# An expert stage whose rows run in passes of 64 and 32: one pass of 32 for experts with few rows, bias rows loaded by another engine, and the work between the passes regrouped

## The chip, the cores and the metric

The kernel runs on one core of one Trainium2 chip. The metric is the device time of the core in microseconds (us). Three runs of the kernel before gave 1849.51 to 1851.67 us, median 1851.08.

Engines are named as in the profile: PE is the matmul engine (PEld its weight loads, PEq its sequencer, which also takes the branches and the waits), DVE the vector engine, ACT the scalar engine, POOL the general engine, SP the engine that issues most DMAs.

## What is computed

One decoder layer over 512 tokens of width 1024. A dense part comes first (a token mixer and a cross-attention, each with a LayerNorm) and does not change. Then a mixture of experts and a last LayerNorm:

```
logits = x @ w_router + b_router            # 512 x 32
top_val, top_idx = top_k(logits, 4)         # every token goes to 4 of 32 experts
gate = softmax(top_val)
for each expert e, over its own tokens xi:
    gu = xi @ w_gu[e] + b_gu[e]             # 1024 -> 2048, interleaved gate and linear part
    h  = min(g,7) * sigmoid(1.702*min(g,7)) * (clip(l,-7,7) + 1)
    y[token] += gate * (h @ w_dn[e] + b_dn[e])
out = layer_norm(alpha * x + y)
```

How many rows an expert has follows from the inputs. With the inputs of the reference, in the order of the experts: 49, 68, 94, 45, 50, 119, 41, 117, 131, 65, 9, 83, 52, 80, 73, 31, 73, 22, 27, 67, 85, 38, 45, 42, 144, 15, 147, 49, 58, 72, 21, 36. So 6 experts have up to 32 rows (10, 15, 17, 18, 25 and 30), 11 have 33 to 64, 12 have 65 to 128, 3 have 129 to 160, and none has more.

## The kernel before

The 512 KB slabs of the experts' weights (16 for the up projection and 8 for the down projection of each expert) stream through a ring of 36 buffers; SP issues them in the order in which they are used, each as soon as its buffer is free. The rows of an expert are the stationary side of the matmuls, in groups of 64 or 32 columns, and the slabs stream past them, 512 columns at a time. Groups of 64 run two at a time on the array, groups of 32 four at a time.

`up` goes through the eight slab pairs in four quarters (`q`). Each quarter is a chain of nested branches on a register that holds the expert's row count: a pass of 64 for rows 0 to 63 always, a pass of 32 for rows 64 to 95 if there are over 64, another for rows 96 to 127 if over 96, and a pass of 64 for rows 128 to 191 if over 128. `down` does the same in two halves. In this text a block is one such chain with its branches, so an expert has four blocks of `up`, two of `down`, and one in `hidden`, which transposes the activated units in the same nested way.

The program is one long list without a loop; the instructions of experts that are not needed are jumped over. Where a branch skips matmuls, the path that skips them goes by a wait of PE for its own semaphore ("waits PE_49" in the listings below, EVENT_SEMAPHORE in the trace), so that all paths leave the block with the same count.

The order around it, for each `e`: the four quarters of `up(e)`, with hooks between them (`turn_units`: the transposes of `hidden` for expert `e-1`; `next_slots`: the routing matmuls `sl` for expert `e+2`), then the first half of `down(e-1)`, then `units(e)` on DVE and ACT and on PE the transposes of the next expert's tokens (`tokens`, tile `xt`, copied by ACT to `xe`), the second half of `down(e-1)`, and at last `rows_out(e-1)` and an indirect DMA that adds the rows to `based`. This order is written out by hand.

The bias of `up` is a matmul at the end of the fourth quarter, with `bgu` as its moving side. `bias_rows` builds `bgu` once before the first expert: two halves of 128 x 1024 are loaded, and each is split on ACT and DVE in a chain of casts and subtractions (tiles `bguraw` and `bgu`).

Of the kernel before, what the change touches and what calls it, by code (L numbers as in the profile page):

```python
# [111 lines left out]
class Trunk:  # L112
# [541 lines left out]

    def layer_norm(self, z, out, gb, add=None, keep=False):
# [4 lines left out]
        for i in range(2):  # L660
            nc.vector.bn_stats(st[:, i, :], half(z, i))
        nc.vector.bn_aggr(mv[:, 0:2], st)
        self.rstd_col(mv[:, 2:3], mv[:, 1:2])
        nc.vector.scalar_tensor_tensor(mv[:, 3:4], mv[:, 0:1], -1.0, mv[:, 2:3], op0=OP.mult, op1=OP.mult)
        for i in range(2):
            v = half(z, i)
            nc.scalar.activation(v, v, AF.Identity, bias=mv[:, 3:4], scale=mv[:, 2:3])
            u = half(out, i) if keep else v
            nc.vector.tensor_mul(u, v, half(gb[0], i))  # L669
            (add or nc.vector).tensor_add(half(out, i), u, half(gb[1], i))  # L670

# [401 lines left out]
    def tokens(self, rv):  # L1073

        nc, tc = self.nc, self.tc
        x = self.mx.tile([128, 8, 192], F32, name="xe", tag="xe", bufs=1)

        def some(c, n, src, first=0):
            nc.scalar.copy(x[:, :, c:c + n], self.turned(src, 8, "xt", first).rearrange("p (k t) -> p k t", t=n))  # L1079

        some(0, 64, self.xg[0:64])
        with tc.If(rv > 64):  # L1082
            some(64, 64, self.xg[64:128], 64)
            with tc.If(rv > 128):
                some(128, 64, self.more_x)
        return x
# [50 lines left out]
    def units(self, rv, b, bm, twice, between):  # L1137

        tc = self.tc
        g = self.mx.tile([128, 512], F32, name="mg", tag="mg", bufs=1)  # L1140
        l, l2, lx = [self.mx.tile([128, 512], F32, name=n, tag=n, bufs=1) for n in ("ml", "ml2", "mlx")]
        with tc.If(rv > 128):
            self.some_units(g, lx, *bm)
        self.some_units(g, l, b[0], b[1], twice)
        between()
        with tc.If(rv > 64):
            self.some_units(g[0:64], l2[0:64], b[2][0:64], b[2][64:128])
            with tc.If(rv > 96):
                self.some_units(g[64:128], l2[64:128], b[3][0:64], b[3][64:128])
        return l, l2, lx  # L1150

    def hidden(self, rv, l, l2, lx):

        nc, tc = self.nc, self.tc
        hs = self.mx.tile([128, 8, 192], F32, name="hs", tag="hs", bufs=1)

# [4 lines left out]
        some(0, 64, l)  # L1161
        with tc.If(rv > 64):  # L1162
            some(64, 32, l2[0:64])
            with tc.If(rv > 96):  # L1164
                some(96, 32, l2[64:128], 64)
                with tc.If(rv > 128):
                    some(128, 64, lx)
        return hs
# [12 lines left out]

    def down(self, rv, h, w, middle):
        tc = self.tc
        y, y2 = [self.ps("y", "y") for _ in range(2)]
        y3, yx = [self.ps("yx", "gu") for _ in range(2)]
        for q in range(2):
            ks = range(4 * q, 4 * q + 4)
            self.down_64(ks, y, h[:, :, 0:64], w)
            with tc.If(rv > 64):
                self.down_32(ks, y2, h[:, :, 64:96], w)  # L1190
                with tc.If(rv > 96):  # L1191
                    self.down_32(ks, y3, h[:, :, 96:128], w)
                    with tc.If(rv > 128):
                        self.down_64(ks, yx, h[:, :, 128:192], w)
            if q == 0:
                middle()
        return y, y2, y3, yx

    def rows_out(self, rv, few, p, route):

        nc, tc = self.nc, self.tc
        self.ys.reverse()
        y = self.ys[0]
        yx = self.mx.tile([64, 1024], F32, name="ysx", tag="ysx", bufs=1)
        gate = route[0][1]
# [7 lines left out]

        with tc.If(rv > 64):
            with tc.If(rv > 96):
                with tc.If(rv > 128):
                    for n in range(2):
                        t = yx[:, ts(n, 512)]
                        nc.scalar.copy(t, p[3][64 * n:64 * n + 64])
                        nc.scalar.mul(t, t, route[1][1])  # L1220
                sums(slice(96, 128), p[2])
            sums(slice(64, 96), p[1])
        nc.vector.tensor_copy(y[0:64, 0:512], p[0][0:64])
        nc.scalar.copy(y[0:64, 512:1024], p[0][64:128])  # L1224
        self.scatter(y, route[0][0])
# [3 lines left out]
    def bias_rows(self):  # L1229
# [3 lines left out]
        for h in range(2):  # L1233
            raw = p.tile([128, 2, 512], F32, name="bguraw", tag=("ysx", "hs")[h], bufs=1)
            for i in range(4):
                nc.sync.dma_start(raw[32 * i:32 * i + 32], self.a["bgu"][:, ts(h, 1024)].rearrange("e (j c) -> e j c", j=2))
            nc.vector.tensor_scalar(raw[:, 1], raw[:, 1], 1.0, None, op0=OP.add)
            t = p.tile([128, 2, 512], BF, name="bgu", tag="bgu", bufs=2)
            nc.scalar.copy(t, raw)
            for first in (32, 64):  # L1240
                for r in (slice(a, a + 32) for a in range(first, 96, 32)):
                    nc.vector.tensor_sub(raw[r], raw[r], t[r])
                    nc.scalar.copy(t[r], raw[r])
            self.bgu.append(t)

    def cond(self, c, *engines):
# [3 lines left out]
    def experts(self):  # L1250
        nc, tc, a = self.nc, self.tc, self.a
        p, cond = self.mx, self.cond
        PE, DVE, ACT, POOL = (mybir.EngineType.PE, mybir.EngineType.DVE, mybir.EngineType.Activation, mybir.EngineType.Pool)
        self.more_x = p.tile([64, 1024], F32, name="mrxg", bufs=1)
        nc.vector.memset(self.more_x, 0.0)
        self.ys = [p.tile([128, 1024], F32, name=f"ysb{i}", bufs=1) for i in range(2)]
        for y in self.ys:
            nc.vector.memset(y, 0.0)

# [21 lines left out]
        def more_gather(e):  # L1281
            with tc.If(rv[e][2] > 128):
                self.gather(self.more_x, route[e][1][0])

# [8 lines left out]
        n = len(self.ring["s"][0])  # L1293
        fetch(24)
        self.bias_rows()
        fetch(n - 24)
        more_gather(0)
        xs, ls = {0: self.tokens(rv[0][0])}, {}
        with tc.manual_schedule(engines={PE, DVE, ACT, POOL}):
            for e in range(33):  # L1300
# [29 lines left out]
                def own_units(between):  # L1330
                    if e < 32:
                        ls[e] = self.units(rv[e][1], *own, route[e][2], between)
                    else:
                        between()

                if e < 32:
                    own = self.up(rv[e][3], e, xs.pop(e), lambda h, k: slabs[e, h, k], {0: [turn_units], 1: [first_slots], 2: [next_slots]})
# [11 lines left out]
    def overflow(self):  # L1349
# [4 lines left out]
        with tc.If(rv > CAP):  # L1354
# [52 lines left out]
            with tc.For_i(0, total, 1):  # L1407
# [52 lines left out]
                y = p.tile([128, 1024], F32, name="oy", tag="ysx", bufs=1)  # L1460
                for n in range(2):
# [15 lines left out]
    FP = 0, 2  # L1477

    NRAW = 8, 14, 5
    W0, KF, MID = 2, 0, 6  # L1480
# [43 lines left out]
```

## Time and profile before

| what | value |
| --- | --- |
| median of three runs | 1851.08 us (1849.51 to 1851.67) |
| profiled execution, its own time | 1848.75 us |
| its span, from the first to the last instruction | 1847.0 us |
| dense part, up to the first matmul of `up(0)` | 615.4 us |
| `up(0)` to the first matmul of `up(1)` | 35.0 us |
| from there to the end of the last `down` | 1160.1 us |
| the rest: last rows, last LayerNorm, output | 36.5 us |
| PE busy over the span | 1673.8 us (91%) |
| mean DMA rate over the span | 273 GB/s |

The profiled execution took 1.75 us more than its span (what lies before the first and after the last instruction), and it lies 2.3 us under the median of the three runs.

### The profile page before, as it was taken

How to read it: one execution, taken by the hardware profiler on the slowest of the kernel's cores; microseconds unless marked ns; L12 is line 12 of the kernel's file. 1: busy time of each engine (PE TensorE's matmuls, PEld its weight loads, DVE VectorE, ACT ScalarE, POOL GpSimd, SP SyncE). 2: the span in 40 equal slices, each digit the busy share in tenths (PEclk: the TensorE clock that was granted, in tenths of full speed). 3: DMA queues.
4: the chain of work that ended last, by engine and by line, in shares of the span. 5: the costliest groups of instructions: out<-in, count | busy, mean ns of one | idle time of the engine just before them, and what ended most of it. 6: DMA issues, size and time to landing. Idle time of an engine off the chain costs nothing. (4 is left out here: it accounts for less than half of the span.)

```text
span 1847.0 us, 26521 instructions
## 1 busy us (share of the span) xinstructions
PE 1673.8 (91%) x9564; PEld 853.2 (46%) x9564; DVE 625.5 (34%) x1322; ACT 469.8 (25%) x906; POOL 293.9 (16%) x402
## 2 busy tenths in 40 slices
PE   8999999999999688999999989899999999999991
PEld 7766877868987333333333333333333333333330
DVE  7855777567565411111111211111112102121114
ACT  5577655335443211101101201110101101111001
POOL 1010002421002211211101121111111211011102
PEclk9999999999999799999999999999999999999996
DMA  5223323675236999999858899999999999678973
GB/s 171 91 69 109 105 81 123 221 225 173 83 123 219 351 391 346 396 374 383 305 186 267 325 375 395 364 372 382 392 401 382 376 392 354 229 284 328 399 270 120
DMA packets 149256, 504.87 MB, mean 273 GB/s; under 512 B 21648, under 2 KB 24240, under 8 KB 149040
## 3 DMA queue, kind: packets, MB, share of 16 engines
q1 hardware_dynamic: 131152, 459.33, 66.2%
q0 software_dynamic: 17024, 40.97, 7.6%
q8 instruction: 149, 2.44, 0.5%
q10 hardware_dynamic: 864, 1.57, 0.2%
q14 instruction: 67, 0.55, 0.1%
HBM read 486.84 MB, written 33.29 MB: 282 GB/s over the span
## 5 line engine op out<-in xcount | busy, mean ns | idle before, releaser
L1098 PE MATMUL gu<-raw,xe 128*64 128x512 f32 (+1 forms) x2624 | 518.0, 601 | 27.8 <-PEq L1191 5.1
L1098 PEld LDWEIGHTS gu<-raw,xe 128*64 128x64 f32 (+1 forms) x2624 | 158.2, 127 | 319.8 <-issue 292.9
L1173 PE MATMUL y<-raw,hs 128*64 128x512 f32 x920 | 211.1, 597 | 17.1 <-PEq L1121 4.3
L1133 ACT ACTIVATE mg<-mg 128x512 f32<-128x512 f32 (+1 forms) x55 | 34.7, 630 | 528.8 <-DVE mg L1132 524.4
L1012 DVE TENSOR_REDUCE gs<-sl 128x1 f32<-128x3 f32 x32 | 5.1, 161 | 478.3 <-PE sl L1010 478.3
L998 POOL TENSOR_SCALAR oh<-places,pm 128x192 bf16<-128x192 bf16 x128 | 98.7, 800 | 387.9 <-PE sl L1010 375.8
L1173 PEld LDWEIGHTS y<-raw,hs 128*64 128x64 f32 x920 | 71.1, 136 | 126.5 <-issue 91.1
L130 DVE TENSOR_TENSOR wlo<-raw,whi 128x1024 fp32r<-128x1024 f32 (+2 forms) x81 | 86.9, 1075 | 45.8 <-ACT whi L130 45.3
L1031 POOL DMA_INDIRECT based<-ysb,ixm x32 | 51.5, 1611 | 292.5 <-ACT ysb L1224 280.2
L130 ACT CAST whi<-raw 128x1024 fp32r<-128x1024 f32 (+2 forms) x81 | 75.3, 932 | 81.9 <-issue 17.3
L1098 PE MATMUL gu<-wlo,xe 128*64 128x512 f32 (+1 forms) x368 | 87.5, 594 | 3.1 <-PEq L1164 1.7
L1098 PE MATMUL gu<-whi,xe 128*64 128x512 f32 (+1 forms) x336 | 79.3, 599 | 7.5 <-DVE ysb L1211 2.1
L1025 POOL DMA_INDIRECT xg<-x2d,ixm x32 | 35.9, 1121 | 313.3 <-PEq L1082 179.3
L1132 DVE TENSOR_SCALAR mg<-gu 128x512 f32<-128x512 f32 (+1 forms) x52 | 35.8, 688 | 126.9 <-PE gu L1090 122.8
L1079 ACT COPY xe<-xt 128x512 f32<-128x512 f32 x50 | 27.8, 588 | 190.5 <-PE xt L1070 190.5
L1180 PE MATMUL y<-raw,hs 128*32 128x512 f32 x440 | 57.6, 598 | 0.0
L1211 DVE TENSOR_TENSOR ysb<-ysb,y 32x512 f32<-32x512 f32 x30 | 20.4, 680 | 103.1 <-ACT ysb L1210 103.0
L162 PE MATMUL g<-xTh,wlo 128*128 128x512 f32 x128 | 52.1, 407 | 2.8 <-DVE wlo L130 2.8
L1158 ACT COPY hs<-ht 128x512 f32<-128x512 f32 (+1 forms) x55 | 26.5, 510 | 106.8 <-PEq L1162 56.2
L160 PE MATMUL g<-xTh,whi 128*128 128x512 f32 x128 | 52.2, 408 | 0.0
L161 PE MATMUL g<-xTl,whi 128*128 128x512 f32 x128 | 51.8, 405 | 0.0
L1098 PEld LDWEIGHTS gu<-wlo,xe 128*64 128x64 f32 (+1 forms) x368 | 25.2, 125 | 49.0 <-issue 47.1
(495 smaller groups left out, 2776.9 us busy)
## 6 DMA issues: line engine op xcount, KB each, us to landing
raw<-in_wgu SPq DMA_DIRECT2D x406, 512.0 KB
raw<-in_wdn SPq DMA_DIRECT2D x230, 512.0 KB
wlo<-in_wgu SPq DMA_DIRECT2D x53, 512.0 KB
whi<-in_wgu SPq DMA_DIRECT2D x53, 512.0 KB
raw<-in_wt SPq DMA_DIRECT2D x27, 512.0 KB
whi<-in_wdn SPq DMA_DIRECT2D x13, 512.0 KB
wlo<-in_wdn SPq DMA_DIRECT2D x13, 512.0 KB
tgd<-tg POOLq DMA_DIRECT2D x16, 256.0 KB, 3.5
```

Source lines behind the costliest of these rows:

```text
L130: return nc.scalar.copy(hi, src).ins, (lo_eng or nc.vector).tensor_sub(lo, src, hi.bitcast(F32)).ins
L160: mm(out, w[0], x[0], start=start, stop=False)
L161: mm(out, w[0], x[1], start=False, stop=False)
L162: mm(out, w[1], x[0], start=False, stop=stop)
L998: self.nc.gpsimd.tensor_scalar(oh[:, b], self.places, self.pm[:, b, e:e + 1], None, op0=OP.is_equal)
L1025: return self.nc.gpsimd.indirect_dma_start(out=xg, out_offset=None, in_=self.x2d, in_offset=bass.IndirectOffsetOnAxis(ap=ix[:, 0:1], axis= ...
L1031: self.nc.gpsimd.indirect_dma_start(out=self.based, out_offset=bass.IndirectOffsetOnAxis(ap=ix[:, 0:1], axis=0), in_=y, in_offset=None, bo ...
L1098: mm(out(h, j), x[:, k], w(h, k)[:, ts(j, 512)], start=k == 0, stop=False)
L1132: nc.vector.tensor_scalar(g, pg, 7.0, None, op0=OP.min)
L1133: nc.scalar.activation(g, g, AF.Gelu_apprx_sigmoid)
L1173: self.nc.tensor.matmul(o[64 * n:64 * n + 64], h[:, k], w(k)[:, ts(n, 512)], start=k == 0, stop=k == 7)
L1180: self.nc.tensor.matmul(o[r:r + 32], h[:, k], w(k)[:, ts(n, 512)], start=k < 2, stop=k > 5)
```

## The change

It has six parts.

1. `up`, `units`, `hidden`, `down` and `rows_out` get an outer branch on 32 rows. Above 32 the nested passes run as before; up to 32 a single pass of 32 runs in the `Else`.
2. Rows 128 to 159 run in a pass of 32 (a further one up to 191) in place of one pass of 64.
3. From `e = 1` on, `turn_units` and `next_slots` both run after the second quarter of `up`; they ran after the first and the third.
4. `units` and the next expert's token transposes run ahead of `down`; they ran between its halves.
5. `bias_rows` loads its rows from ACT's queue and not from SP's, comes ahead of all 36 slabs and not behind the first 24, and its first half uses the tile `ysb`. Tiles `ysb`, `more_x` and `ysx` are merged, and the ring grows by two slabs (`NRAW`).
6. The last LayerNorm takes the sums of blocks 1 and 3 on ACT (`sums`), and all its last additions run on DVE; those of blocks 0 and 2 ran on POOL.

```diff
 def up(...):
     for q in range(4):
         ks = (2 * q, 2 * q + 1)
-            self.up_part(e, ks, 64, x[:, :, 0:64], w, two(b))
-            with tc.If(rv > 64):
-                self.up_part(e, ks, 32, x[:, :, 64:96], w, four(b[2]))
-                with tc.If(rv > 96):
-                    self.up_part(e, ks, 32, x[:, :, 96:128], w, four(b[3]))
-                    with tc.If(rv > 128):
-                        self.up_part(e, ks, 64, x[:, :, 128:192], w, two(bm))
+            with tc.If(rv > 32) as some:
+                self.up_part(e, ks, 64, x[:, :, 0:64], w, two(b))
+                with tc.If(rv > 64):
+                    self.up_part(e, ks, 32, x[:, :, 64:96], w, four(b[2]))
+                    with tc.If(rv > 96):
+                        self.up_part(e, ks, 32, x[:, :, 96:128], w, four(b[3]))
+                        with tc.If(rv > 128):
+                            self.up_part(e, ks, 32, x[:, :, 128:160], w, four(bm[0]))
+                            with tc.If(rv > 160):
+                                self.up_part(e, ks, 32, x[:, :, 160:192], w, four(bm[1]))
+            with some.Else():
+                self.up_part(e, ks, 32, x[:, :, 0:32], w, four(b[0]))
...
 def down(...):
-            self.down_64(ks, y, h[:, :, 0:64], w)
-            with tc.If(rv > 64):
+            with tc.If(rv > 32) as some:
+                self.down_64(ks, y, h[:, :, 0:64], w)
+                with tc.If(rv > 64):
...
-            if q == 0:
-                middle()
+            with some.Else():
+                self.down_32(ks, y, h[:, :, 0:32], w)
...
 def bias_rows(self):
-            raw = p.tile([128, 2, 512], F32, name="bguraw", tag=("ysx", "hs")[h], bufs=1)
+            raw = p.tile([128, 2, 512], F32, name="bguraw", tag="hs", bufs=1) if h else self.ys.rearrange("p (j c) -> p j c", j=2)
             for i in range(4):
-                nc.sync.dma_start(raw[32 * i:32 * i + 32], self.a["bgu"][:, ts(h, 1024)].rearrange("e (j c) -> e j c", j=2))
+                nc.scalar.dma_start(raw[32 * i:32 * i + 32], self.a["bgu"][:, ts(h, 1024)].rearrange("e (j c) -> e j c", j=2))
...
 def experts(self):
-        fetch(24)
         self.bias_rows()
-        fetch(n - 24)
+        fetch(n)
...
+                hooks = {1: [turn_units, next_slots]} if e else {0: [turn_units], 1: [first_slots], 2: [next_slots]}
...
-                    out = self.down(rv[f][3], h[f], lambda k: slabs[f, 2, k], lambda: own_units(next_tokens))
+                    own_units(next_tokens)
+                    out = self.down(rv[f][3], h[f], lambda k: slabs[f, 2, k])
...
 def finish(self):
-                self.layer_norm(z, out[b], gb, nc.gpsimd if b in self.FP else None)
+                self.layer_norm(z, out[b], gb, stats=self.sums if b % 2 else None)
...
+    def sums(self, mv, z, scratch):
+        nc = self.nc
+        nc.scalar.activation(scratch, z, AF.Identity, accum_out=mv[:, 0:1])
+        nc.vector.tensor_scalar(mv[:, 3:4], mv[:, 0:1], -1.0 / 1024, None, op0=OP.mult)
+        nc.scalar.activation(scratch, z, AF.Square, bias=mv[:, 3:4], accum_out=mv[:, 1:2])
+        nc.vector.tensor_scalar(mv[:, 0:1], mv[:, 3:4], -1.0, None, op0=OP.mult)
+        nc.vector.tensor_scalar(mv[:, 1:2], mv[:, 1:2], 1.0 / 1024, None, op0=OP.mult)
```

What the change makes of the program is seen at two places. The first is one block of `up` on PE. Before, it is this (64x512 is the pass of 64, 32x512 one of 32, `gux` the rows from 128 on; L1119, L1121 and L1123 are the branches on 64, 96 and 128 rows, and a row with "waits PE_49" is the skipping path of that branch):

```order
L1119 COMPARE_AND_BRANCH
L1098 MATMUL gu<-raw,xe 32x512 [waits DVE_49]
L1098 MATMUL gu<-raw,xe 32x512 x7
L1121 COMPARE_AND_BRANCH
L1098 MATMUL gu<-raw,xe 32x512 x8
L1123 COMPARE_AND_BRANCH
L1098 MATMUL gux<-raw,xe 64x512 x8
L1123 UNCONDITIONAL_BRANCH
L1123 UNCONDITIONAL_BRANCH [waits PE_49]
L1121 UNCONDITIONAL_BRANCH [waits PE_49]
L1119 UNCONDITIONAL_BRANCH [waits PE_49]
```

The eight matmuls of rows 0 to 63 stand ahead of these rows without a branch, and the last row is also the end of the block. After the change, the same block of PE ends like this (L1131 is the new branch on 32 rows, L1139 the one on 160, `gux` now in 32x512):

```order
L1139 COMPARE_AND_BRANCH
L1110 MATMUL gux<-raw,xe 32x512 x8
L1139 UNCONDITIONAL_BRANCH
L1139 UNCONDITIONAL_BRANCH [waits PE_49]
L1137 UNCONDITIONAL_BRANCH [waits PE_49]
L1135 UNCONDITIONAL_BRANCH [waits PE_49]
L1133 UNCONDITIONAL_BRANCH [waits PE_49]
L1110 MATMUL gu<-raw,xe 32x512 [waits DMAHW0_49]
L1110 MATMUL gu<-raw,xe 32x512 [waits DMAHW2_49]
L1110 MATMUL gu<-raw,xe 32x512 x2
L1131 UNCONDITIONAL_BRANCH
```

A branch on 32 rows (L1131) now stands at the head of the block, and behind the paths for more rows lie eight matmuls for up to 32 rows, which those paths must jump over; the path of the eight matmuls itself has no wait of PE for its own semaphore.

The second place is ACT's program just ahead of `up(0)`. Before, behind the four DMAs that write `based` comes the copy of the first expert's tokens (`xe<-xt`, on which the first matmul of `up(0)` waits), and the bias rows' casts come later:

```order
L1048 DMA based<-x2g 128x512 [waits DMAHW1_49,DVE_49]
L1079 COPY xe<-xt 128x8x64 [waits PE_49]
L1282 UNCONDITIONAL_BRANCH
L1247 TENSOR_LOAD number [waits Pool_49]
L1082 COMPARE_AND_BRANCH
L1084 COMPARE_AND_BRANCH
```

After the change, ACT has these rows in that place (DMAHW0 to DMAHW7 are semaphores of DMAs, shared by turns; the four `based` DMAs use DMAHW6, 7, 0 and 1):

```order
L1060 DMA based<-x2g 128x512 [waits DMAHW1_49,DVE_49]
L1266 DMA ysb<-in_bgu 32x1024 [waits DMAHW2_49,DMAHW6_49,DMAHW1_49,DMAHW0_49]
...
L1266 DMA ysb<-in_bgu 32x1024 [waits DMAHW7_49]
L1266 DMA ysb<-in_bgu 32x1024
L1266 DMA bguraw<-in_bgu 32x1024 [waits DMAHW3_49,Activation_49]
L1266 DMA bguraw<-in_bgu 32x1024 [waits DMAHW5_49]
L1269 CAST bgu<-ysb 128x1024 [waits DMAHW2_49,DMAHW7_49,DMAHW1_49,DVE_49]
L1266 DMA bguraw<-in_bgu 32x1024 [waits DMAHW0_49]
L1273 CAST bgu<-ysb 32x1024 [waits DVE_49] x2
L1266 DMA bguraw<-in_bgu 32x1024 [waits DMAHW3_49]
L1273 CAST bgu<-ysb 32x1024 [waits DVE_49]
L1091 COPY xe<-xt 128x8x64 [waits PE_49]
```

The loads of both halves and the whole chain of casts of the first half now stand ahead of the copy of the first expert's tokens, and the first load waits for the `based` DMAs.

## Rows read from the trace of the kernel before

**Rows 1.** Windows of core 0: busy time (instructions) by engine, PE clock, DMA share, GB/s.

```profile
615.40:650.40 35.00, 21.93 (x116) 8.37 (x117) 13.50 (x24) 10.86 (x12) 8.30 (x11) 0.79 1.01 374
650.40:1810.50 1160.10, 1066.11 (x6492) 374.55 (x6492) 190.46 (x401) 135.93 (x240) 177.51 (x207) 1.00 0.91 344
1810.50:1847.00 36.50, 0.00 (x0) 0.00 (x0) 18.32 (x29) 6.55 (x9) 11.35 (x13) 0.56 0.35 127
```

**Rows 2.** PE's waits from 650.4 to 1810.5: total us, times, longest us.

```profile
PE sl L1007 <- PEq L1121: 6.2, 10, 0.8
PE gu L1098 <- PEq L1121: 4.1, 9, 0.5
...
PE gu L1098 <- DMA raw<-in_wgu: 1.5, 4, 0.5
```

**Rows 3.** PE's timeline in experts 9 and 10: start, us, what, [idle before <-releaser].

```profile
1034.71 3.65 PE L1098 MATMUL gu<-raw,xe 128*64 128x512 f32 x16 [0.16 <-PEq L1119]
...
1047.60 1.92 PE L1180 MATMUL y<-raw,hs 128*32 128x512 f32 x16
```

**Rows 4.** Branch and semaphore instructions of the branch on 64 rows: count, ns min/median/max, first and last start.

```profile
L1119 PEldq COMPARE_BRANCH  x128: 65/208/3248, 618.0 to 1789.2; - x128
L1119 PEldq EVENT_SEMAPHORE  x68: 51/51/51, 622.4 to 1793.2; - x68
```

**Rows 5.** The page's DMA queue of instruction fetches: packets, MB, share of 16 engines.

```profile
q8 instruction: 149, 2.44, 0.5%
```

**Rows 6.** PE's timeline in `up(2)` (94 rows), one quarter.

```profile
701.48 5.51 PE L1098 MATMUL gu<-raw,xe 128*64 128x512 f32 x32 [0.46 <-PEq L1121]
```

**Rows 7.** PE's timeline in `up(8)` (131 rows), where a quarter ends.

```profile
939.06 3.65 PE L1098 MATMUL gux<-raw,xe 128*64 128x512 f32 x16
942.65 0.47 PE L1007 MATMUL sl<-VT,oh 128*128 128x8 bf16 x8
...
```

**Rows 8.** PE's timeline in `up(8)`, its transposes.

```profile
920.43 0.46 PE L1070 MATMUL ht<-ident,ml 64*128 64x64 f32 x4 [0.35 <-ACT hs L1158]
```

**Rows 9.** ACT's timeline around the start of `up(0)`.

```profile
610.13 4.43 ACTq L1048 DMA_DIRECT2D based<-x2g  x4
614.81 0.59 ACT L1079 COPY xe<-xt 128x512 f32<-128x512 f32 x1 [4.48 <-PE xt L1070]
632.89 1.04 ACT L1239 CAST bgu<-bguraw 128x1024 bf16<-128x1024 f32 x1 [17.50 <-DVE bguraw L1237]
...
638.95 1.04 ACT L1243 CAST bgu<-bguraw 32x1024 bf16<-32x1024 f32 x1 [1.28 <-DVE bguraw L1242]
```

**Rows 10.** DVE's timeline there.

```profile
619.03 0.91 DVE L1258 MEMSET ysb<- 128x1024 f32 x1 [3.14 <-DMA based<-x2g]
...
632.41 0.41 DVE L1237 TENSOR_SCALAR bguraw<-bguraw 128x512 f32<-128x512 f32 x1
```

**Rows 11.** PE's timeline there.

```profile
615.45 5.24 PE L1098 MATMUL gu<-raw,xe 128*64 128x512 f32 x10 [0.68 <-ACT xe L1079]
...
632.10 3.65 PE L1098 MATMUL gu<-raw,xe 128*64 128x512 f32 x16 [0.21 <-issue]
640.04 0.38 PE L1090 MATMUL gu<-bgu,esel 128*64 128x512 bf16 x1 [4.29 <-ACT bgu L1243]
647.00 1.01 PE L1090 MATMUL gu<-bgu,esel 128*64 128x512 bf16 x3 [6.58 <-ACT bgu L1243]
...
650.42 7.33 PE L1098 MATMUL gu<-raw,xe 128*64 128x512 f32 x32 [0.54 <-ACT xe L1079]
```

**Rows 12.** Windows as in rows 1: experts 10 to 23, and `up(18)` with `down(17)`.

```profile
1025.60:1487.10 461.50, 417.52 (x2518) 149.69 (x2514) 77.59 (x172) 56.12 (x99) 83.45 (x100) 1.00 1.00 382
...
1299.00:1325.90 26.90, 24.58 (x136) 9.52 (x137) 5.64 (x13) 3.55 (x7) 5.77 (x7) 1.00 1.02 395
```

**Rows 13.** The timeline of the last LayerNorm.

```profile
1826.33 1.25 POOL L670 TENSOR_TENSOR fo<-fz,gain 128x512 f32<-128x512 f32 x1
...
1841.17 0.69 DVE L670 TENSOR_TENSOR fo<-fz,gain 128x512 f32<-128x512 f32 x1
```

More of the change, by code (lines that the diff above doesn't have):

```diff
@@ L653, in gains, with layer_norm @@
         return t
-    def layer_norm(self, z, out, gb, add=None, keep=False):
+    def layer_norm(self, z, out, gb, keep=False, stats=None):
         nc = self.nc
@@ L659, in layer_norm @@
         mv = self.pst.tile([128, 4], F32, name="mv", tag="mv")
-        for i in range(2):
-            nc.vector.bn_stats(st[:, i, :], half(z, i))
-        nc.vector.bn_aggr(mv[:, 0:2], st)
+        if stats:
+            stats(mv, z, out)
+        else:
+            for i in range(2):
+                nc.vector.bn_stats(st[:, i, :], half(z, i))
+            nc.vector.bn_aggr(mv[:, 0:2], st)
         self.rstd_col(mv[:, 2:3], mv[:, 1:2])
@@ L669, in layer_norm @@
             nc.vector.tensor_mul(u, v, half(gb[0], i))
-            (add or nc.vector).tensor_add(half(out, i), u, half(gb[1], i))
+            nc.vector.tensor_add(half(out, i), u, half(gb[1], i))
+    def sums(self, mv, z, scratch):
[5 more added lines that the diff above has]
+        nc.vector.tensor_scalar(mv[:, 1:2], mv[:, 1:2], 1.0 / 1024, None, op0=OP.mult)
     def transpose_tok(self, x, b, xT):
@@ L1084, in tokens @@
             with tc.If(rv > 128):
-                some(128, 64, self.more_x)
+                some(128, 64, self.more[64:128], 64)
         return x
@@ L1142, in units @@
         with tc.If(rv > 128):
-            self.some_units(g, lx, *bm)
-        self.some_units(g, l, b[0], b[1], twice)
+            nc.vector.memset(lx[64:128], 0.0)
+            self.some_units(g[0:64], lx[0:64], bm[0][0:64], bm[0][64:128])
+            with tc.If(rv > 160):
+                self.some_units(g[64:128], lx[64:128], bm[1][0:64], bm[1][64:128])
+        with tc.If(rv > 32) as some:
+            self.some_units(g, l, b[0], b[1], twice)
+        with some.Else():
+            self.some_units(g[0:64], l[0:64], b[0][0:64], b[0][64:128])
         between()
@@ L1159, in some @@
                            self.turned(src, 4, "ht", first).rearrange("p (j h t) -> p j h t", j=4, h=2))
-        some(0, 64, l)
-        with tc.If(rv > 64):
[L1163 to L1167, printed above, removed]
+        with tc.If(rv > 32) as more:
+            some(0, 64, l)
+            with tc.If(rv > 64):
+                some(64, 32, l2[0:64])
+                with tc.If(rv > 96):
+                    some(96, 32, l2[64:128], 64)
+                    with tc.If(rv > 128):
+                        some(128, 32, lx[0:64])
+                        some(160, 32, lx[64:128], 64)
+        with more.Else():
+            some(0, 32, l[0:64])
         return hs
@@ L1180, in down_32, with down @@
                 self.nc.tensor.matmul(o[r:r + 32], h[:, k], w(k)[:, ts(n, 512)], start=k < 2, stop=k > 5)
-    def down(self, rv, h, w, middle):
+    def down(self, rv, h, w):
         tc = self.tc
@@ L1187, in down @@
             ks = range(4 * q, 4 * q + 4)
-            self.down_64(ks, y, h[:, :, 0:64], w)
[L1189 to L1194, printed above, removed]
-            if q == 0:
-                middle()
+            with tc.If(rv > 32) as some:
+                self.down_64(ks, y, h[:, :, 0:64], w)
+                with tc.If(rv > 64):
+                    self.down_32(ks, y2, h[:, :, 64:96], w)
+                    with tc.If(rv > 96):
+                        self.down_32(ks, y3, h[:, :, 96:128], w)
+                        with tc.If(rv > 128):
+                            self.down_64(ks, yx, h[:, :, 128:192], w)
+            with some.Else():
+                self.down_32(ks, y, h[:, :, 0:32], w)
         return y, y2, y3, yx
@@ L1201, in rows_out @@
         nc, tc = self.nc, self.tc
-        self.ys.reverse()
-        y = self.ys[0]
-        yx = self.mx.tile([64, 1024], F32, name="ysx", tag="ysx", bufs=1)
+        y, yx = self.ys, self.more[0:64]
         gate = route[0][1]
@@ L1212, in sums @@
             nc.vector.tensor_scalar(y[r], y[r], gate[r], None, op0=OP.mult)
[L1214 to L1224, printed above, removed]
+        with tc.If(rv > 32) as some:
+            with tc.If(rv > 64):
+                with tc.If(rv > 96):
+                    with tc.If(rv > 128):
+                        for n in range(2):
+                            t = yx[:, ts(n, 512)]
+                            nc.scalar.copy(t, p[3][64 * n:64 * n + 64])
+                            nc.scalar.mul(t, t, route[1][1])
+                    sums(slice(96, 128), p[2])
+                sums(slice(64, 96), p[1])
+            nc.vector.tensor_copy(y[0:64, 0:512], p[0][0:64])
+            nc.scalar.copy(y[0:64, 512:1024], p[0][64:128])
+        with some.Else():
+            sums(slice(0, 32), p[0])
         self.scatter(y, route[0][0])
@@ L1244, in bias_rows @@
             self.bgu.append(t)
+        nc.vector.memset(self.ys, 0.0)
     def cond(self, c, *engines):
@@ L1253, in experts @@
         PE, DVE, ACT, POOL = (mybir.EngineType.PE, mybir.EngineType.DVE, mybir.EngineType.Activation, mybir.EngineType.Pool)
[L1254 to L1258, printed above, removed]
+        self.more = p.tile([128, 1024], F32, name="more", bufs=1)
+        self.ys = p.tile([128, 1024], F32, name="ysb", bufs=1)
+        nc.vector.memset(self.more, 0.0)
         order = []
@@ L1282, in more_gather @@
             with tc.If(rv[e][2] > 128):
-                self.gather(self.more_x, route[e][1][0])
+                self.gather(self.more[64:128], route[e][1][0])
         def routing(e):
```

9 lines of the change are left out of this document (4 added, 5 removed).

## The prediction

> **What bounds the kernel now.** I read the windows by stage first. The dense part is the same in both kernels. In the expert stage PE is busy 1066 of 1160 us at a clock of 1.00, while DVE and ACT are busy a sixth and an eighth [rows 1]. Then PE's waits in that stage: behind data they are tiny (1.5 us in all for a matmul of `up` behind a slab), and the longer ones name PE's own sequencer, PEq, that is branches and semaphores [rows 2]. So the stage lasts as long as PE's passes plus the gaps between blocks, and I cost the change by these two. A third place is the start: around `up(0)` the window's clock is 0.79 and PE waits for the bias rows [rows 1, 11]. The windows also show a DMA share of 1.00 over experts 10 to 23 [rows 12]: the slabs come just in time there, which makes a rival below.
>
> **Prices.** A pass of 64 over a quarter of `up`, or a half of `down`, takes 3.65 us, a pass of 32 takes 1.92 [rows 3]: 1.73 apart. The pass of 64 is eight pairs that follow each other by about 0.44 us (3.65 less the 0.59 of the last, over seven). Where a block of up to 64 rows ends, PE idles 0.16 us behind the last matmul's end [rows 3], so start follows start by 0.75 us instead of 0.44: the drain costs 0.31. That path passes the semaphore wait on the branch on 64 rows, 68 times, four for each of 17 experts [rows 4]. Where a block of 65 to 96 rows ends, PE idles 0.46 us [rows 6], since that path must also jump over the next path's rows. Where all passes run (over 128) there is no idle time at all: 942.65 follows a pass that ends at 942.71 [rows 7]. A branch takes between 65 and 3248 ns, median 208 [rows 4].
>
> **The change part by part**, in us against the profiled execution:
>
> *Up to 32 rows, 6 experts: -55.* Six blocks, each 1.73 shorter, are 10.4. Their path has no wait of PE for itself, so six times 0.31 of drain goes too: 12.3 for an expert, 74 for six. Against that, each block now begins with a jump over all the larger passes, seven per expert with the transposes, 42 in all. A jump is hidden as long as matmuls are queued, here 1.92 us of them where before there were 3.65; the longest branch took 3.25, so a stall is between 0 and 1.33 us, 0 to 56 in all. I take 0.45 per jump, nearer to the median (208 ns, covered) than to the longest: 19. The term lies between -74 and -18.
>
> *33 to 64 rows, 11 experts: +33.* The same passes, but this path now ends like that of 65 to 96 rows, with a drain and a jump over the `Else`: 0.46 in place of 0.16. And every block begins with a branch not taken that comes right behind a drain, with nothing queued to hide it: at least 0.065, at most the median 0.208, I take 0.13. That is 0.43 for each of seven blocks (four, two, and `hidden`), 3.0 for an expert. Bounds +23 (the jump alone) to +39. A gain is excluded, for no matmul is removed.
>
> *65 to 128 rows, 12 experts: +8.* They only get that branch at the head of seven blocks: 84 times 0.065 to 0.208, +5.5 to +17; I take 0.1, since part of them follow blocks whose drain is longer.
>
> *Over 128 rows, 3 experts: -8.* Four passes of 64 become passes of 32: -6.9. But these blocks had no drain and no jump [rows 7], and now have both, about 0.6 in each of seven: +4.2. Net -2.7 each; between -21 (if blocks stay without gaps) and -8.
>
> *Transposes and slots in one place: +4.5.* The number of borders between kinds of work stays the same. But the slots now follow the transposes at once, and both use the same PSUM tiles, whose release is ACT's copy `hs`; such a wait took 0.35 [rows 8]. For 15 experts with over 64 rows 0.3 each; 0 to +9.
>
> *Tokens ahead of `down`: +2.* PE's own work is the same. The copies `xe` now have all of `down` as cover (at least 3.5 us) instead of half. A third transpose (three experts) waits for a copy that stands behind ACT's activation: 0.6 each; 0 to +4. If the cover were gone, a copy of 0.59 [rows 9] would show in front of `up`.
>
> *Bias rows: +4.5.* Now PE waits for them at the end of `up(0)`: 4.29 and 6.58 us, the last bias matmul ends at 648.0 [rows 11]. The chain could not start earlier than 632.4 because DVE had the slots' work in front of it in its order [rows 10]. That stall goes, and so does the slow start of `up(1)`: 7.33 us for a pass of 64 and one of 32 [rows 11] against 5.51 warm [rows 6], -1.8. In its place `up(0)` starts late. The first load waits for the last write of `based`: issued by 614.6 and landed by 619.0, when DVE's memset could start [rows 9, 10], so 4.4 us to land. I take four issues until 620.6 and 4.4 more: 625.0. The first half's chain took from 632.41 to 639.99 [rows 9, 10], 7.6: 632.6. Only then comes the copy `xe` in ACT's order, and the first matmul 0.64 after its start [rows 9, 11]: 633.2 instead of 615.45. From there to the end of the last quarter it was 20.3 (615.45 to 635.75) [rows 11]: 653.5, and 654.3 with the four bias matmuls, 6.3 later than 648.0. With -1.8 this is +4.5. SP's slabs no longer queue behind the bias loads, but the ring is full before PE starts, so that gains nothing. Bounds +1 (rows landing in 2 us) to +12 (8 us later, behind slabs that share the DMA engines).
>
> *Last LayerNorm: 0.* Two blocks' additions leave POOL (1.25 us each) for DVE (0.69) [rows 13], and four statistics leave DVE; but block 3's sums on ACT stand in order behind three blocks' scaling. Played through with the rows' durations the last addition ends within 0.5 us of the 1841.9 of before; -2 to +2. The merged tiles cost nothing as long as a scatter has landed when the next expert's rows are written, an expert's time later; a late one would add the rest of its landing.
>
> Sum: -55 + 33 + 8 - 8 + 4.5 + 2 + 4.5 + 0 = -11, from 1848.75 to 1837.7. The profiled execution lies 2.3 under the median of the three runs, so the time to compare with 1851.08 is **1840**.
>
> **Rivals.**
>
> *Instruction fetch sets the pace of the small experts; slower.* The program is fetched in 149 packets of 2.44 MB, 16 KB each [rows 5]. A block of `up` jumps over some 40 matmuls with their loads, and single branches took up to 3.25 us [rows 4]; before, 3.65 us of queued work hid them all. If every jump shows its full 1.33, the small experts gain 18 instead of 55: the sum is +26, 1877. It decides from 0.71 us per jump on (0.45 + 11/42), and the kernel is measurably slower from 0.80 on. A half-way case, 0.9 per jump, gives 1859. For it: the longest branch; against it: a median of 0.208 and small gaps in [rows 2].
> [...]
>
> *Drains and branches cost little.* If the new jumps over the `Else` and the branches at the heads are hidden, the third and fourth terms nearly vanish: -11 - 33 - 8 = -52, 1799; with half of them -31, 1820. Against it: blocks of 65 to 96 rows show their 0.46 without fail (longest in one place 0.5) [rows 2, 6].
>
> *Slabs become the bound.* `up(18)` with `down(17)` takes 26.9 us at a DMA share of 1.02 and 395 GB/s [rows 12]; after the change it takes some 16.5 for the same 24 slabs, 12.6 MB, which alone need 32 at that rate. The ring holds 36 to 38 slabs, some 48 us, ahead. Over experts 10 to 23 PE would need about 443 us (37 less for four small experts, 18 more for the ten others), the slabs 14 x 32 = 448. So they are hidden as long as the ring is well filled at expert 10, for the largest deficit, that of experts 17 and 18, is some 22 us; with a ring half empty some 10 us of the gain are lost: 1850.
>
> **How the numbers follow.** The signs of the terms are hardly in doubt, their sizes are. Forecast (-2 to -22): 0.42. Drains and branches cheap (-22 to -50): 0.24. Fetch-bound small experts, with the half-way case (+0 to +27): 0.24. Slabs bound or a late start of `up(0)` at its upper bound (-4 to +6): 0.10. From 1840 the range reaches to both sides until 2 in 10 are left: 1814 to 1863. A difference under 0.2%, 3.7 us, can't be told from none. Faster by more: all of the cheap case, nine tenths of the forecast, a fifth of the rest: 0.64. Within: 0.13. Slower: 0.23.
>
> **What would show it.** In the timeline of PE: `up(10)` with four passes of 1.92 us and gaps under 0.5 between them (the stall per jump is read there); blocks of `up(3)` (45 rows) with idle times of about 0.6 in place of 0.16; `up(8)`'s blocks with gaps; the first matmul of `up(0)` at 633, no wait at the bias matmuls, `up(1)` at 656.5. In the waits: no more time behind slabs than 2 us. The prediction is wrong if jumps stall by over 0.8 us, if the outer branch is hidden, or if the bias loads take 8 us longer to land.

## The result and the profile after

The changed kernel takes 1956.3 us (median of four runs, 1949.5 to 1962.2) against 1850.5 for the kernel before (median of four runs, too): ratio 1.057, 95% interval 1.055 to 1.059. That is 106 us slower, far outside the range, which ended at 1863. Its profiled execution has a span of 1950.9 us.

The windows of after, cut at the same places as [rows 1] (up(0) to up(1), from there to the last `down`, the end), show where:

```profile
630.90:656.80 25.90, 20.22 (x116) 7.25 (x116) 7.78 (x18) 7.09 (x8) 8.52 (x11) 0.88 1.03 400
656.80:1915.70 1258.90, 1044.05 (x6504) 344.97 (x6504) 200.12 (x415) 134.96 (x249) 181.64 (x207) 0.93 0.85 317
1915.70:1950.90 35.20, 0.04 (x2) 0.00 (x0) 14.85 (x33) 11.11 (x17) 4.59 (x9) 0.57 0.43 155
```

The expert stage has grown from 1160 to 1259 us while PE's busy time in it fell by 22. PE is now idle for 215 us of it, and the granted clock is 0.93, where it was 1.00. The slabs are not it: the DMA share fell from 0.91 to 0.85.

In PE's waits of that stretch (total, times, longest) the largest is one that the profile can't name, and stalls of several microseconds appear:

```profile
PE gu L1110 <- issue: 28.0, 26, 3.9
PE gu L1110 <- DMA raw<-in_wdn: 18.5, 16, 3.9
PE sl L1019 <- ACTq L1189: 11.4, 8, 6.8
```

In the kernel before the same kind of wait was the largest too, but none of the 28 was longer than 0.4 us; [rows 2] starts with the line behind this one:

```profile
PE gu L1098 <- issue: 6.6, 28, 0.4
```

(A matmul of `up` needs no slab of `in_wdn`: where the profile finds no releaser it names the last event.) PE's timeline of `up(18)`, 27 rows, shows the small pass itself:

```profile
1361.80 1.92 PE L1110 MATMUL gu<-raw,xe 128*32 128x512 f32 x16 [2.27 <-issue]
...
1368.16 3.22 PE L1110 MATMUL gu<-raw,xe 128*32 128x512 f32 x16 [2.61 <-DMA wlo<-in_wdn]
1373.93 3.39 PE L1110 MATMUL gu<-raw,xe 128*32 128x512 f32 x16 [2.55 <-DMA raw<-in_wdn]
```

The pass of 1.92 us is there, as forecast, but the last two start 5.77 us apart, with 2.5 us of nothing in front of each, and they are slower (3.2 and 3.4 us): the mean granted clock is 0.59 and 0.55 while they run; it was 1.00 up to 1366, before PE's idle time of 2.61 us. What PE does in the gap is seen in the branch at the head of the block, among the instructions of its line in after (count, then min, median and max in ns, first and last start):

```profile
L1131 PEldq COMPARE_BRANCH  x128: 70/73/6350, 618.6 to 1893.4; - x128
```

It takes up to 6.35 us where it jumps over the larger passes (in `up(10)`, 9 rows). What it waits for moves on the queue of PE's instruction fetches, in the page of after (packets, MB, share of 16 engines' span; [rows 5] is the same line of before):

```profile
q8 instruction: 198, 3.24, 0.7%
```

PE's program has grown from 149 packets of 16 KB to 198. The same queue in the DMA view of the 32 us of `up(18)` with `down(17)`, 1357.6 to 1389.6:

```profile
q8 instruction: 6, 0.10, 1.2%
```

Six packets arrive in that time, though PE executes no more than 138 matmuls and as many weight loads in it, and a packet holds some 258 instructions (51133 in 198 packets). The same stretch of the kernel before took 26.9 us [rows 12].

The traces of the runs also hold the start and the duration of every packet, and these tie the long branches to the fetch. In `up(18)` the branch on 32 rows takes 2.17 us from 1365.83 and 5.53 us from 1368.23, ahead of the two late passes; each time one packet lands, at 1366.58 and at 1372.33, and the branch ends 1.4 us later. It is so with all 36 branches of PE over 1.2 us in after: a packet has landed 1.1 to 1.5 us before the end. In before 16 branches are that long, 31 us in all, in after 36 with 131 us (part of it under matmuls that were still queued: the branch from 1357.68 took 3.95 us, and PE was idle for 2.27 before its next pass, at 1361.80).

### The profile page after: what moved, and what is told of

It is laid out like the page before. It is cut to its first block, busy times and chain, and to the rows that moved or that the text cites. A ratio compares the mean times of both kernels' runs of the same rounds, so it can differ in the third digit from the quotient of the medians.

```text
span 1950.9 us, 27186 instructions
## 1 busy us (share of the span) xinstructions
PE 1650.4 (85%) x9576; PEld 822.1 (42%) x9576; DVE 630.9 (32%) x1340; ACT 473.4 (24%) x923; POOL 291.6 (15%) x398
## 5 line engine op out<-in xcount | busy, mean ns | idle before, releaser
L1110 PE MATMUL gu<-raw,xe 128*64 128x512 f32 (+1 forms) x2716 | 558.8, 651 | 109.5 <-issue 27.2
L1201 PE MATMUL y<-raw,hs 128*64 128x512 f32 x676 | 160.9, 614 | 25.0 <-DMA raw<-in_wgu 8.0
L1151 ACT ACTIVATE mg<-mg 64x512 f32<-64x512 f32 (+1 forms) x55 | 34.6, 630 | 476.2 <-DVE mg L1150 460.8
L1201 PEld LDWEIGHTS y<-raw,hs 128*64 128x64 f32 x676 | 51.0, 139 | 116.1 <-issue 73.8
L1208 PE MATMUL y<-raw,hs 128*32 128x512 f32 x544 | 81.6, 667 | 15.2 <-DMA raw<-in_wgu 6.7
L1182 ACT COPY hs<-ht 128x256 f32<-128x256 f32 (+1 forms) x58 | 25.5, 470 | 280.1 <-PE ht L1082 180.2
L1110 PE MATMUL gu<-wlo,xe 128*32 128x512 f32 (+1 forms) x304 | 72.6, 608 | 9.5 <-DVE ysb L1238 2.1
L1110 PE MATMUL gu<-whi,xe 128*32 128x512 f32 (+1 forms) x308 | 75.6, 625 | 2.9 <-DMA raw<-in_wgu 1.3
L1237 ACT COPY ysb<-y 32x512 f32<-32x512 f32 x42 | 24.3, 578 | 167.0 <-PE y L1208 146.0
L1208 PEld LDWEIGHTS y<-raw,hs 128*32 128x32 f32 x544 | 17.3, 116 | 67.8 <-issue 66.2
```

The lines of the kernel that those rows point to most:

```text
L1110: mm(out(h, j), x[:, k], w(h, k)[:, ts(j, 512)], start=k == 0, stop=False)
L1151: nc.scalar.activation(g, g, AF.Gelu_apprx_sigmoid)
L1201: self.nc.tensor.matmul(o[64 * n:64 * n + 64], h[:, k], w(k)[:, ts(n, 512)], start=k == 0, stop=k == 7)
L1208: self.nc.tensor.matmul(o[r:r + 32], h[:, k], w(k)[:, ts(n, 512)], start=k < 2, stop=k > 5)
```

## The experiments

Theory: PE's program comes in 16 KB packets, one after the other, executed or not; a PE that jumps ahead waits some 5.3 to 5.8 us per packet (six packets in the 32.0 us of `up(18)` with `down(17)`, its two late passes 5.77 us apart). So an expert can't be shorter than its code. That the packets come in the order of the program is my assumption; no trace shows it. Rivals: the drains and branches by themselves, the new order of units, tokens and slots, the late `up(0)`, the slabs.

| run | time, us | ratio to before, 95% |
| --- | --- | --- |
| e1_dead | 1893.3 | 1.022 (1.020 to 1.024) |
| e5_dead_half | 1866.9 | 1.009 (1.007 to 1.011) |
| e4_small_only | 1886.9 | 1.018 (1.016 to 1.020) |
| e2_no_else | 1874.7 | 1.014 (1.010 to 1.018) |
| e3_hooks | 1935.1 | 1.044 (1.043 to 1.046) |
| e6_mid | 1958.0 | 1.058 (1.056 to 1.061) |
| e7_tokens_first | 1955.3 | 1.057 (1.054 to 1.060) |
| c1_after_cap160 | 1878.5 | 1.015 (1.013 to 1.017) |
| c2_mid | 1864.2 | 1.006 (1.004 to 1.008) |
| c3_small_cap160 | 1858.9 | 1.004 (1.002 to 1.006) |
| b1_cap160 | 1808.7 | 0.977 (0.975 to 0.979) |
| b2_halves | 1781.8 | 0.962 (0.961 to 0.964) |
| b3_pool | 1802.0 | 0.973 (0.972 to 0.975) |
| b4_halves_pool | 1782.2 | 0.963 (0.962 to 0.965) |
| b5_down_one | 1790.8 | 0.968 (0.966 to 0.970) |

**Code that never runs, in the kernel before** (e1_dead; e5_dead_half has only the first of the two passes in `up`):

```diff
                     with tc.If(rv > 128):
                         self.up_part(e, ks, 64, x[:, :, 128:192], w, two(bm))
+                        with tc.If(rv > 400):
+                            self.up_part(e, ks, 32, x[:, :, 128:160], w, four(bm[0]))
+                            self.up_part(e, ks, 32, x[:, :, 160:192], w, four(bm[1]))
...
                         self.down_64(ks, yx, h[:, :, 128:192], w)
+                        with tc.If(rv > 400):
+                            self.down_32(ks, yx, h[:, :, 128:160], w)
```

> The kernel before, plus matmuls that never run (behind a branch on 400 rows, inside the branch on 128 rows), so that PE's program grows from 38712 to 50040 instructions, about what the change makes of it (51133), while the executed work stays the same. Theory (instruction fetch): PE's program is fetched in sequence, 16 KB after 16 KB, executed or not, and a stalled PE gets one such packet per 5.7 us or so; with 5.3 packets per expert instead of 4.0 no expert can take less than some 30 us, and those that took 26 to 31 are stretched: 1866 to 1890 us. Rival (drains and branches cost by their own execution, not by the code they skip): 1851 to 1855 us.

> As e1_dead, with some 60% of its unexecuted matmuls (45629 instructions on PE, 4.8 packets per expert). Fetch theory with a floor per expert: 27 us or so, which only the shortest experts reach: 1858 to 1872 us, clearly less than 60% of the 41 us that e1_dead lost. Rival (a fixed cost per fetched packet, hidden nowhere): 60% of it, 1875 to 1880 us.

Without one more executed matmul the kernel loses 41 us (against 1852.6 for the kernel before), 3 more than the upper end of what was expected, and with 60% of that code it loses 16 (against 1851.2), as expected. The code is fetched although nobody executes it; the page of e1_dead has

```profile
q8 instruction: 194, 3.18, 0.7%
```

packets, where that of before has 149. These windows are `up(4)` and `up(20)`, each with the `down` before it, first in the kernel before, then in e1_dead:

```profile
759.30:786.40 27.10, 24.74 (x136) 9.54 (x137) 5.62 (x13) 3.54 (x7) 5.90 (x7) 1.00 1.03 395
1361.50:1402.00 40.50, 36.04 (x232) 11.91 (x232) 5.10 (x12) 3.74 (x7) 5.84 (x7) 1.00 1.00 389
```

```profile
763.50:795.10 31.60, 26.29 (x138) 10.04 (x139) 5.70 (x13) 3.50 (x7) 5.90 (x7) 0.95 1.03 394
1384.40:1424.50 40.10, 36.06 (x234) 11.98 (x234) 5.13 (x12) 3.81 (x7) 5.84 (x7) 1.00 0.98 359
```

The short row (a row here is the stretch from an expert's first matmul of `up` to the next expert's) is stretched from 27.1 to 31.6 us, the long one isn't. It is a floor for short rows more than a cost per packet, and the half dose says so too: 16 us are 39% of 41, not 60%, and the five rows that took under 28 us before, those with `up` of experts 4, 18, 22, 23 and 28, are 16 us longer in e1_dead and 4 in e5_dead_half. The floor isn't all of it: some 14 of the 41 us lie in the rows of experts 8, 9 and 24 to 27, long ones that hold the three large experts, and there the added branch on 400 rows is itself executed. The branch that was there before now waits up to 6.1 us (3.2 in [rows 4]), on code that nobody executes:

```profile
L1119 PEldq COMPARE_BRANCH  x128: 65/212/6092, 620.1 to 1834.0; - x128
```

**The first part alone, and the change without it.** e4_small_only is the kernel before with the outer branch on 32 rows in `up`, `units`, `hidden`, `down` and `rows_out`; e2_no_else is the changed kernel without them:

```diff
-            with tc.If(rv > 32) as some:
-                self.up_part(e, ks, 64, x[:, :, 0:64], w, two(b))
-                with tc.If(rv > 64):
...
-            with some.Else():
-                self.up_part(e, ks, 32, x[:, :, 0:32], w, four(b[0]))
+            self.up_part(e, ks, 64, x[:, :, 0:64], w, two(b))
+            with tc.If(rv > 64):
...
```

> The kernel before with the first part of the change alone (outer branch on 32 rows, one pass of 32 up to 32 rows; 46131 instructions on PE). Fetch theory: the small experts gain nearly nothing, since their code (4.9 packets per expert) is fetched no faster, and the others pay for drains, jumps and stalls: 1890 to 1925 us. Rival (my forecast's terms, -55 + 33 + 8): 1834 to 1842 us.

> The changed kernel without its first part: no outer branch on 32 rows and no pass of 32 for small experts (43715 instructions on PE). Fetch theory: 4.6 packets per expert, some 26 us, are nearly hidden again and the drains of the outer branch are gone; what is left is the later start of up(0) (+6), slots that wait behind the transposes (+10 to +20) and the shorter passes beyond 128 rows (-12): 1853 to 1872 us. Rival (the loss comes from the new order of units, tokens and slots): above 1920 us.

The first part alone costs 34 us, where my terms for it made -14; I had expected 3 us more at the least. Taking it out of the changed kernel gives back 82, more than it costs alone, so the parts don't simply add. That the parts share the same fetched code, and that one uncovers stalls which the other leaves under cover, is my reading of it and not shown by itself. e2 ended 3 us above what was expected.

**The new order.** e3_hooks sets `hooks` back to `{0: [turn_units], 1: [first_slots], 2: [next_slots]}`, e6_mid puts units and tokens back between the halves of `down`, e7_tokens_first calls `tokens(0)` ahead of `bias_rows`:

```diff
-        self.bias_rows()
-        fetch(n)
         more_gather(0)
         xs, ls = {0: self.tokens(rv[0][0])}, {}
+        self.bias_rows()
+        fetch(n)
```

> The changed kernel with the transposes and the slots again after the first and the third quarter of up. Theory (the slots stand behind the transposes' copies on ACT, which stand behind the rows of the expert before): 15 to 25 us come back, 1930 to 1942 us. Rival (these waits only take the place of others, since the fetch sets the pace): within 5 us of 1956.

> The changed kernel with units and the next tokens' transposes again between the halves of down. Theory (that move costs nothing of its own): within 8 us of 1956. Rival (the copies of the tokens and the activations now come too late for up, because nothing of down lies in front of them): 10 us or more faster.

> The changed kernel with the first expert's tokens ahead of the bias rows in the program, so that ACT copies them first. Theory (the first matmul of up(0) waited only for that copy): up(0) starts at 615 to 616 again and PE waits some 5 us for the bias rows at its end; 8 to 14 us less than 1956. Rival (the late start is hidden behind slabs and fetches later): no more than 3 us.

The slots behind the transposes cost 21 us, as expected: the wait `sl <- ACTq L1189` (up to 6.8 us, above) is gone from e3's waits. The place of the tokens costs nothing in this kernel. e7 missed: `up(0)` did start earlier, at 619.7 and not at 631, but PE then waited for the bias rows, whose loads on ACT's queue came later, and `up(1)` began at 657.6, where it was 656.8:

```profile
619.69 4.50 PE L1110 MATMUL gu<-raw,xe 128*64 128x512 f32 x9 [4.69 <-POOL oh L1010]
...
643.22 0.38 PE L1102 MATMUL gu<-bgu,esel 128*64 128x512 bf16 x1 [2.61 <-ACT bgu L1273]
653.72 1.01 PE L1102 MATMUL gu<-bgu,esel 128*64 128x512 bf16 x3 [10.12 <-ACT bgu L1273]
...
657.62 7.90 PE L1110 MATMUL gu<-raw,xe 128*64 128x512 f32 x32 [0.78 <-ACTq L1096]
```

**Less code.** In these, rows from 160 on go to the overflow loop that the kernel has (`CAP` 160 in place of 192), and rows 128 to 159 take one pass of 32 in `up` and in `down` (shown against the kernel before):

```diff
-CAP = 192
+CAP = 160
...
-                        self.up_part(e, ks, 64, x[:, :, 128:192], w, two(bm))
+                        self.up_part(e, ks, 32, x[:, :, 128:160], w, four(bm))
...
-                        self.down_64(ks, yx, h[:, :, 128:192], w)
+                        self.down_32(ks, yx, h[:, :, 128:160], w)
```

c1_after_cap160 is the changed kernel with this and e3's edit, c2_mid has e6's too, c3_small_cap160 is e4_small_only with it.

> The changed kernel with rows from 160 on left to the overflow loop, one pass of 32 in down for rows 128 to 159, and transposes and slots after the first and third quarter again; PE's program shrinks from 51133 to 46098 instructions, that of e4_small_only. Fetch theory: e4's 1887, less 38 for the three large experts as in b1_cap160, plus some 5 for the bias rows: 1848 to 1862 us. Rival (the changed order of units and tokens costs by itself): above 1880.

> c1_after_cap160 with units and the next tokens' transposes again between the halves of down. Theory (two short halves in a row leave no work under which the next code packet arrives): 12 to 25 us less than 1878. Rival (their place does nothing, as in e6_mid): within 4 us of 1878.

> e4_small_only with rows 128 to 159 in one pass of 32 and rows from 160 on left to the overflow loop (old order, old bias rows). If the terms add: 1887 - 38 = 1849, 1843 to 1855 us. Rival (shorter passes beyond 128 rows uncover more stalls when a small pass exists): 1860 or more.

From 1956 the changed kernel comes to 1878 with the smaller code and the old hooks, and to 1864 with the old place of units and tokens. So that place does matter there (14 us), and I take it that larger stalls cover it in the changed kernel. c1 came out 16 us above the upper end of what I expected, and c3 4 above: the terms don't simply add. No version with the small pass beats the kernel before.

**Versions that do.** b1_cap160 is the kernel before with the diff above, bias rows loaded by ACT behind the first tokens, and the changed last LayerNorm. b2_halves has `up` in two blocks:

```diff
-        for q in range(4):
-            ks = (2 * q, 2 * q + 1)
+        for q in range(2):
+            ks = range(4 * q, 4 * q + 4)
...
-{0: [turn_units], 1: [first_slots], 2: [next_slots]}
+{0: [turn_units], 1: [first_slots, next_slots]}
```

b3_pool loads the bias rows by `nc.gpsimd.dma_start`, b4_halves_pool is both, and b5_down_one is b2 with `down` in one block behind units and tokens.

> A version meant to beat both: the kernel before; rows 128 to 159 in one pass of 32 in up and down, and rows from 160 on left to the overflow loop that exists (CAP 160 in place of 192), so that PE's program does not grow (38676 instructions); bias rows loaded by ACT's queue, written behind the first tokens; the changed LayerNorm at the end. Theory: 3 experts x (6.9 + 3.4) = 31 us less, 7 to 9 for the bias rows, 1 for the end: 1808 to 1818 us. Rival (what the passes save is lost to slabs or fetches): above 1835.

> b1_cap160 with up in two blocks of four slab pairs each instead of four of two; transposes after the first, slots after the second. Theory (a block's end costs 0.31 us of drain up to 64 rows and 0.6 above): two ends less for each of 32 experts, -25 to -29: 1780 to 1786 us. Rival (longer jumps run out of the fetched code, and slabs are freed later): no better than 1805.

> b1_cap160 with the bias rows loaded by POOL's own queue, whose semaphores SP's slabs do not share. Theory (on ACT's queue the last loads waited for semaphores of slabs): the wait in front of the bias matmuls falls from 9.6 us to 2 to 5, 1801 to 1806 us. Rival (POOL's loads land no earlier): within 2 us of 1808.7.

> Both edits of b2_halves and b3_pool on b1_cap160. They touch different stretches, so their gains should add: 1773 to 1784 us.

> b2_halves with down in one block of eight slabs, and units and tokens ahead of it. Theory (one block's end less per expert, 0.31 or 0.6 us): -10 to -14, 1767 to 1773 us. Rival (a jump now skips up to 1.1 packets with less queued in front, or the slabs become the bound): 1780 or more.

b1 gains 42 us; the rows of experts 8, 9 and 24 to 27, which hold the three large experts, became 38 us shorter in all. b2 is the best, about 70 us faster than the kernel before (1852.4 beside it): the ends of blocks are dear, 27 us for two per expert, as worked out from the drains of [rows 3, 6]. Its page has

```profile
q8 instruction: 147, 2.41, 0.5%
```

packets, two fewer than before, so nothing is paid back in fetches. b1 to b4 all came out within what was expected. b3's gain at the start (7 us) did not show in b4, though `up(1)` began 8 us earlier there than in b2 (650.9 and 659.0). By the two timelines the rows of experts 12 and 18 lose 3.3 and 2.6 of it again, at a mean clock of 0.95 and 0.94; what started that is open.

b5 is 9 us slower than b2 and missed what was expected. Its branch in `down` waits longer (up to 4.6 us where b2's is 2.9), but that isn't where most of the time went: most rows are 0.3 to 0.9 us shorter than in b2, and those of experts 7, 23 and 25 are 2.6, 2.7 and 3.9 us longer. The next expert of each of these three has over 128 rows, and PE idles 1.6 us there before the third transpose of its tokens (`xt`). In two of the three places the profile names ACT's copies `xe` as what ended the wait, as in row 7:

```profile
895.82 0.97 PE L1082 MATMUL xt<-ident,mrxg 32*128 32x32 f32 x8 [1.59 <-ACT xe L1091]
```

In b2 PE idles 0.37 us in the same three places. The mean clock of these rows is 1.00 in b2 and 0.92 to 0.96 in b5. These three rows alone lose 9.2 us, so it is mostly the place of the tokens, ahead of `down`, that costs in b5. Whether one block of `down` pays with the tokens in another place was not tried.

## Why the prediction was wrong

*The step that failed* is the bound in "Up to 32 rows, 6 experts: -55": "a stall is between 0 and 1.33 us". I took it from the longest branch before (3.25 us) less the matmuls queued behind it, as if the fetch were the same. But the change raises the number of packets that must pass, from 149 to 198, and that sets the pace of a short expert (in e1_dead the row with `up(4)` went from 27.1 to 31.6 us by it). Stalls went to 6.35 us. By PE's timelines it idles 45 us in front of the 24 passes of `up` of the six small experts in after, 1.9 us for each (0.3 in before), where I took 0.45 for a stall and allowed 1.33 at most. These experts' four blocks of `up`, 6.9 to 8.2 us shorter by my prices before stalls, took 3.4 us more on average, idle time in front of them counted: the shorter passes are eaten up by the stalls and by the lower clock behind them (0.59 and 0.55 in the late passes of `up(18)`). The rival "Instruction fetch sets the pace" named the cause, with 0.24, but its price (1877 at most) rested on the same bound. The traces show that code which is never executed is fetched too (194 packets in e1_dead, 149 before) and that the long branches ended 1.1 to 1.5 us after a packet had landed; how far ahead of PE its program is fetched they don't show.

*The neighbours.* I charged the stall to small experts only. Branches of the other classes waited too (L1133, on 64 rows, up to 4.4 us), and the granted clock was 0.93 on average, with longer passes where it was low: 3.2 and 3.4 us at 0.59 and 0.55 for a pass of 1.92 at 1.00 above. Part 1 alone came to +34 and not -14. By PE's timelines of before and e4_small_only, idle time counted in, `up` and `down` of the small experts became 6 us shorter (forecast 55), those of 33 to 64 rows 18 longer (33), and those of 65 to 128 rows 12 longer (8). In after, with the other parts beside it, all three are longer, by some 26, 30 and 30 us.

*33 to 64 and 65 to 128 rows: +33 and +8.* Right in mechanism, and in size where a block shows it alone. That the class of 33 to 64 rows came to 30 in after is in part luck: of 22.5 us in `up` only 11 are idle time, the rest are passes at a lower clock, for which there was no term. `up(3)` (45 rows) of after:

```profile
743.61 3.65 PE L1110 MATMUL gu<-raw,xe 128*64 128x512 f32 x16 [0.56 <-PEq L1133]
```

0.56 against 0.16 in [rows 3]; forecast 0.59. The rival "Drains and branches cost little" fails by that, and b2's 27 us show it from the other side.

*Over 128 rows: -8.* Their rows became 3 to 7 us shorter each, about 15 in all: within the bounds, and about twice the forecast.

*Transposes and slots: +4.5, bounds 0 to +9.* Measured 21 (e3). I took the wait for ACT's copies from a place where ACT was free (0.35); here the copies stand in ACT's order behind `rows_out` of the expert before, and PE waited for them up to 6.8 us.

*Tokens ahead of `down`: +2.* Zero in the changed kernel (e6), 14 in c1 (c2). The third transpose, which I had priced at 0.6 us for each of three experts, waited 1.6 in b5, where the mean clock of these rows was 0.92 to 0.96 (1.00 in b2); in c1 the rows of experts 7, 23 and 25 are 2.0, 2.0 and 3.9 us longer than in c2, and PE idles 0.6 to 2.2 us in front of `xt` there, of which no wait over 0.5 us is left in c2. What the rest of the 14 is made of is open.

*Bias rows: +4.5.* Right in mechanism. PE's timeline:

```profile
630.95 4.53 PE L1110 MATMUL gu<-raw,xe 128*64 128x512 f32 x9 [17.10 <-ACTq L1094]
...
652.14 0.61 PE L1102 MATMUL gu<-bgu,esel 128*64 128x512 bf16 x4
...
656.83 7.20 PE L1110 MATMUL gu<-raw,xe 128*64 128x512 f32 x32 [0.78 <-DMA wlo<-in_wgu]
```

`up(0)` starts at 631.0 (forecast 633.2), no wait at the bias matmuls, `up(1)` at 656.8 (656.5). The slow start of `up(1)` stayed (7.20 us), so it is +6.4. That `up(1)` hit the forecast is luck: `up(0)` started 2.2 us earlier than forecast, its bias matmuls ended 1.5 earlier (652.8), and the way from there to `up(1)` took some 4 us where I had 2.2.

*Last LayerNorm: 0.* 35.2 us against 36.5, -1.3.

*Slabs as the bound:* not what made it slower; DMA share and rate fell. Whether they would bind if the small experts were as short as forecast, no run shows.

## What to carry to other kernels

Where branches skip code in a program without loops, count what is skipped as well as what is run: divide the packets that the fetch queue shows by the stage's units of work, and compare that, times the spacing of packets where the engine waits for them (5.4 to 6.4 us here), with the shortest unit. As I read these runs, a second path for the small case pays only while the short unit stays longer than the code it must pass (six packets and 32.0 us in `up(18)` with `down(17)`, for which I had forecast some 16.5); shorter passes for the large experts and fewer blocks, with no more code, gave 70 us here where the special path lost 34. And a wait borrowed from the trace before held only where the engine that ends it had the same work in front: PE waited 0.35 us for ACT's copies in before and up to 6.8 in after.

## What the runs showed of the hardware that was not expected

A PE that jumped ahead got a 16 KB packet about every 5.4 to 6.4 us (the six packets that start from 1365.6 to 1395.1 in after), and of the 168 gaps between packets in its expert stage 157 are 5.3 us or longer, the shortest 3.1. Yet a packet itself takes 1.0 us at the median and 1.9 at most: most of that spacing is not the packet's own time. A branch that waited for a packet ended 1.1 to 1.5 us after it had landed. What sets the spacing is open; the 16 DMA engines were full meanwhile (share 1.02 in `up(18)` with `down(17)`, 0.93 of it on the queue that carries the slabs), and no run is without slabs.
